# GpSimd's weight splits and stick-weight products cut into shorter instructions

## The chip, the cores and the metric

The kernel runs on one core of one Trainium2 chip. The metric is the device time of one execution in microseconds; the median of three runs before the change is 2070.41 us (2069.74 to 2076.77). Engines are named as the profile names them: PE is TensorE's matmul side, PEld its weight loads, DVE is VectorE, ACT is ScalarE, POOL is GpSimd, SP is SyncE. Lines such as L339 are lines of the kernel before.

## The reference

One decoder layer over 16 meta tokens and 1024 tokens of width 1024, all in float32:

```
xn   = rms_norm(h, g_pre_mix)
b, c, hc, q, k, v, g_conv, g_attn = split(xn @ w_in)            # 8 x 1024 columns
y    = b * causal_dwconv3(c * hc)
z    = q k^T / 8, strictly causal, 16 heads of 64
A[t,s] = sigmoid(z_ts) * prod_{s<j<t} (1 - sigmoid(z_tj))       # stick breaking
mix  = (sigmoid(g_conv + b0) * (y @ w_proj_conv) + sigmoid(g_attn + b1) * (A v @ w_proj_attn)) @ w_out
h    = h + rms_norm(mix, g_post_mix)
u, g = split(rms_norm(h, g_pre_ffn) @ w_up_gate)                # 2 x 2816 columns
out  = h + rms_norm((gelu(causal_dwconv3(u)) * g) @ w_down, g_post_ffn)
```

## The kernel before

Every product is computed to float32 accuracy from rounded operands: a tensor is split into `hi` (its rounded copy) and `lo` (what the rounding lost), and three matmuls, hi by hi, hi by lo and lo by hi, add up in one PSUM bank. The helper `split` (L63 to L65) does it: ACT copies the source into `hi`, and DVE, or POOL where it is named, subtracts `hi` from the source into `lo`.

The first stage, from about 75 to 1000 us, runs two things through one PE queue. One is the dense product `xn @ w_in`: 64 items of 128 output columns in the class `Dense`, each with three chunks of 342 tokens and 24 matmuls a chunk. `run(i)` first prepares the weights of item i+1 (`prep`, L102 to L110: the 128x1024 weight block `raw`, ACT's `whi`, POOL's `wlo`), asks for the DMA of item i+2, and then issues its own matmuls at L124 to L126. The same class later carries the 16 items of the two branch projections, so `prep` splits 80 weight blocks in all.

The other is the stick-breaking attention: 8 pairs of heads, and for each head three groups (g) of three query blocks of 114 rows. `stage1` (L311) handles the query blocks: a block sees nk = 128 + 114 b keys, b = 0 to 8. PE computes the scores z, ACT writes `fl` = sigmoid(-z/8) and `be` = sigmoid(z/8), and the closure `weights`, put off by one chunk through the list `late`, issues the rest: DVE's scan (L336) turns `fl` in place into the running product from the right, POOL multiplies `be` by it, shifted by one key (L339), POOL masks the last 114 columns (L340, an affine select) and fills a margin with zeros (L345, a memset). There are two buffers of `fl`, so block b+2's sigmoid waits until the product of block b has read its `fl`; there are six of `be`.

`stage2` (L353) consumes the three blocks of a group: PE transposes `be` by 128 keys (L373) into one of two PSUM tiles `tp`, ACT and DVE split it into `ah` and `al`, and PE multiplies these by the values (L363, L364). A transpose can only start when DVE has read the PSUM tile of two transposes earlier. A hand-written loop (L506 on) interleaves the steps of stage1, stage2 and the dense items by a table of costs; it fixes the order in which each engine gets its instructions. Engines work through their queues in that order. Beside these, DVE evacuates PSUM and computes the convolution branch (`conv3`: L197 on ACT, then L198 and L199 on DVE, 1026 columns each).

At the start (0 to 45 us) `start_items` normalises the nine token blocks (L459 on DVE for the first three, L461 on POOL and L462 on DVE for the others), transposes them (L179), and slips in the first two dense items, whose two `wlo` splits come between the second and the third token block.

Of the kernel before, what the change touches and what calls it, by code (L numbers as in the profile page):

```python
# [8 lines left out]
F32 = mybir.dt.float32  # L9
F32R = mybir.dt.float32r  # L10
AF = mybir.ActivationFunctionType
ALU = mybir.AluOpType
# [3 lines left out]
D = 1024  # L16
# [16 lines left out]
def block_kernel(ctx, tc, x, meta_tokens, g_pre_mix, w_in, channels, w_proj_conv,  # L33
                 w_proj_attn, w_out, g_post_mix, g_pre_ffn, w_up_gate, w_down,
                 g_post_ffn, out):
    nc = tc.nc
# [26 lines left out]
    def split(hi, lo, src, lo_engine=None):  # L63
        nc.scalar.copy(hi, src)  # L64
        (lo_engine or nc.vector).tensor_tensor(lo, src, hi.bitcast(F32), op=ALU.subtract)  # L65
# [14 lines left out]
    class Dense:  # L80
# [22 lines left out]
        def prep(self, i):  # L103
            if i < len(self.items) and i not in self.hl:
                self.load(i)
                raw = self.raw.pop(i)
                hi = wpool.tile([P, D], F32R, name="whi", tag="whi")
                lo = wpool.tile([P, D], F32R, name="wlo", tag="wlo")
                split(hi, lo, raw, nc.gpsimd)
                self.hl[i] = (hi, lo)  # L110

        def run(self, i):
# [198 lines left out]
    def stage1(p, h, g):  # L311
        res = []
        qh, ql, kk = QH[p][h], QL[p][h], KK[p][h]
        nk_end = P + QB * (3 * g + 2)
        for b in range(3 * g, 3 * g + 3):
            nk = P + QB * b
            q0 = QB * b
            fl = work.tile([P, NT], F32, name="fl", tag="fl")[:QB]
            be = work.tile([P, NT], F32, name="be", tag="be", bufs=6)[:QB]
            nch = -(-nk // 512)  # L320
            wch = 2 * (-(-nk // (2 * nch)))
            c0 = 0
            while c0 < nk:
                n = min(wch, nk - c0)
                z = ps_z.tile([P, 512], F32, name="z", tag="z")[:QB, :n]
                nc.tensor.matmul(z, qh[:, q0:q0 + QB], kk[:, c0:c0 + n], start=True, stop=False)
                nc.tensor.matmul(z, ql[:, q0:q0 + QB], kk[:, c0:c0 + n], start=False, stop=True)  # L327
                nc.scalar.activation(fl[:, c0:c0 + n], z, AF.Sigmoid, scale=-0.125)  # L328
                nc.scalar.activation(be[:, c0:c0 + n], z, AF.Sigmoid, scale=0.125)
                c0 += n  # L330
                if late:
                    late.pop(0)()
                if c0 < nk:
                    yield n
            def weights(fl=fl, be=be, nk=nk):
                nc.vector.tensor_tensor_scan(fl[:, :nk][:, ::-1], fl[:, :nk][:, ::-1],  # L336
                                             upper[:, NT - nk:][:, ::-1], 1.0,
                                             op0=ALU.mult, op1=ALU.max)
                nc.gpsimd.tensor_tensor(be[:, 0:nk - 1], be[:, 0:nk - 1], fl[:, 1:nk], op=ALU.mult)  # L339
                nc.gpsimd.affine_select(out=be[:, nk - QB:nk], in_=be[:, nk - QB:nk],  # L340
                                        pattern=[[-1, QB]], compare_op=ALU.is_gt, fill=0.0,
                                        base=0, channel_multiplier=1)
                pad = min(P * (-(-nk // P)), nk_end)
                if pad > nk:
                    nc.gpsimd.memset(be[:, nk:pad], 0.0)  # L345

            late.append(weights)
            res.append((be, nk))
            if len(res) == 3:
                units[(p, h, g)] = res  # L350
            yield n
# [676 lines left out]
    for k, _ in enumerate(products(0, *HALF[1], bank_of(ps_o, "po"), evac_u(*HALF[1]))):  # L1028
        if k % 2:
            next(prep, None)  # L1030
# [40 lines left out]
    for i in range(1, len(pairs)):  # L1071
        p, gate = divmod(i, 2)
        if gate:
            conv_gelu(p)
            sets = [products(i, 1, 512, bank, evac_g(p))]
        else:
            sets = [products(i, j0, n, bank, evac_u(j0, n)) for j0, n in HALF]
        for _ in prep:
            pass
        prep = prep_pair(i + 1) if i < last_pair else prep_down_first()  # L1080
        for si, st in enumerate(sets):
            for k, _ in enumerate(st):
                if gate or (7 * si + k) % 2:
                    next(prep, None)
# [45 lines left out]
    for gi, fbs in enumerate(groups):  # L1130
# [14 lines left out]
        for tb in range(8):  # L1145
# [3 lines left out]
            for hf in range(2):  # L1149
                ps = bank()  # L1150
                c = slice(hf * 512, (hf + 1) * 512)
# [6 lines left out]
                a = accs[tb][:, c]  # L1158
# [4 lines left out]
                if last:  # L1163
                    sq = dw.tile([P, 512], F32, name="sq", tag="sq", bufs=2)
                    nc.scalar.activation(sq, a, AF.Square, accum_out=ssqs[tb][:, hf:hf + 1])
                    eng = nc.vector if (tb == 7 and hf) else nc.gpsimd
                    eng.tensor_tensor(a, a, g_post2[:, c], op=ALU.mult)
            next(prep, None)
            if last:
                a, hb, s0 = accs[tb], hbs[tb], ssqs[tb]  # L1170
                nc.vector.tensor_tensor(s0[:, 0:1], s0[:, 0:1], s0[:, 1:2], op=ALU.add)
                r = rstd_of(fsml, s0[:, 0:1], P)
                for hf in range(2):
                    c = slice(hf * 512, (hf + 1) * 512)
# [60 lines left out]
```

## Time and profile before

| | us |
|---|---|
| median of three runs | 2070.41 |
| the profiled execution | 2079.27 |
| its span, first to last instruction | 2077.1 |
| PE busy | 1988.1 (96%) |
| PEld busy | 1860.9 (90%) |
| DVE busy | 1033.7 (50%) |
| ACT busy | 851.9 (41%) |
| POOL busy | 914.8 (44%) |
| POOL, 80 splits of `wlo` | 191.5 |
| POOL, 144 products of L339 | 178.3 |
| DVE, 144 scans of L336 | 228.0 |

Busy times are shares of one profiled execution, the slowest core's; there is one core. A matmul's recorded length (0.32 us for 342 columns) is its passage through the array, and its successor starts some 0.16 us after it, so an idle time recorded ahead of a matmul is a little shorter than the time that was lost. A row of the timeline gives start, length, engine, line, operation and tiles, and in brackets the engine's idle time before it with the work that ended it. The time that an instruction spends on waiting for a resource after it was started is part of its length, so two rows of one shape with different lengths are worth a look.

### The profile page before, as it was taken

The page shows a single profiled execution, that of the slowest core. Times are in us where ns is not written, and L with a number is a line of the kernel's source. Part 1 is how long each engine was busy: PE and PEld are TensorE (multiplying, and loading weights), DVE is VectorE, ACT ScalarE, POOL GpSimd, SP SyncE. Part 2 cuts the span into 40 slices and gives each one's busy share as a digit, 9 for nine tenths or more (in the row PEclk, how much of TensorE's full clock was granted, in tenths as well). Part 3 has the DMA queues.
Part 4 walks back from the last instruction along what each step waited for, and adds up shares of the span by engine and source line. Part 5 has one row for each costly group of instructions (what it writes and reads, how often), then busy time and mean ns, then how long its engine had stood idle before and what let it go on. Part 6 is the DMA issues. An engine that isn't in the chain of part 4 may idle for free.

```text
span 2077.1 us, 30701 instructions
## 1 busy us (share of the span) xinstructions
PE 1988.1 (96%) x12228; PEld 1860.9 (90%) x12228; DVE 1033.7 (50%) x1545; ACT 851.9 (41%) x1771; POOL 914.8 (44%) x764
## 2 busy tenths in 40 slices
PE   5999999999999999999999989979999999999997
PEld 5999999999999999999999989978898899878886
DVE  6445555555555555554232114685444444445546
ACT  4445454545444454545441113354334434412122
POOL 4444444434444444444212551225655656555353
PEclk9999999999999999999999999989999999999999
DMA  3111101111111101111475674313222122253323
GB/s 134 41 51 42 61 31 51 42 41 52 42 51 41 61 32 51 41 48 55 138 231 171 184 189 129 102 54 102 74 90 82 62 102 70 74 182 102 101 81 132
DMA packets 56171, 177.56 MB, mean 85 GB/s; under 512 B 12872, under 2 KB 12872, under 8 KB 56028
## 3 DMA queue, kind: packets, MB, share of 16 engines
q1 hardware_dynamic: 52704, 165.09, 24.5%
q10 hardware_dynamic: 3324, 10.50, 1.6%
q8 instruction: 96, 1.57, 0.3%
q14 instruction: 47, 0.39, 0.1%
HBM read 131.36 MB, written 44.21 MB: 85 GB/s over the span
## 4 chain that ended last, share of the span: by engine, by line
PE 74%; DVE 11%; DMA 6%; ACT 4%; POOL 3%; issue 2%; ACTq 0%; DVEq 0%; POOLq 0%; SPq 0%
PE mm L124 13%; PE mm L125 12%; PE mm L126 12%; PE st L863 6%; PE st L865 5%; PE st L867 5%; PE st L1157 3%; PE st L1155 3%; PE st L1156 3%; PE tp L373 3%; DVE fl L336 3%; PE av L363 2%; PE av L364 2%; DMA xv<-in_x_dram 2%; POOL a_op L65 2%
## 5 line engine op out<-in xcount | busy, mean ns | idle before, releaser
L124 PE MATMUL mm<-xnT,whi 128*128 128x342 f32 (+2 forms) x1536 | 506.8, 330 | 3.6 <-ACT xnT L64 3.6
L125 PE MATMUL mm<-xnT,whi 128*128 128x342 f32 (+2 forms) x1536 | 494.7, 322 | 0.5 <-DVE xnT L65 0.5
L126 PE MATMUL mm<-xnT,wlo 128*128 128x342 f32 (+2 forms) x1536 | 493.0, 321 | 0.0
L339 POOL TENSOR_TENSOR be<-be,fl 114x127 f32<-114x127 f32 (+2 forms) x144 | 178.3, 1238 | 372.3 <-DVE fl L336 350.9
L124 PEld LDWEIGHTS mm<-xnT,whi 128*128 128x128 f32 x1536 | 290.5, 189 | 8.3 <-ACT xnT L64 4.0
L125 PEld LDWEIGHTS mm<-xnT,whi 128*128 128x128 f32 x1536 | 291.1, 190 | 2.1 <-DVE xnT L65 1.0
L126 PEld LDWEIGHTS mm<-xnT,wlo 128*128 128x128 f32 x1536 | 290.5, 189 | 0.0
L336 DVE TENSOR_TENSOR_SCAN fl<-fl,upper 114x128 f32<-114x128 f32 (+2 forms) x144 | 228.0, 1585 | 117.6 <-ACT fl L328 102.8
L65 POOL TENSOR_TENSOR wlo<-raw,whi 128x1024 fp32r<-128x1024 f32 x80 | 191.5, 2394 | 203.5 <-ACT whi L64 203.5
L65 POOL TENSOR_TENSOR a_op<-raw,a_op 128x512 fp32r<-128x512 f32 (+1 forms) x136 | 193.6, 1436 | 88.6 <-ACT a_op L64 86.4
L65 DVE TENSOR_TENSOR al<-tp,ah 128x342 fp32r<-128x342 f32 (+4 forms) x288 | 127.3, 450 | 147.0 <-ACT ah L64 145.7
L64 ACT CAST ah<-tp 128x342 fp32r<-128x342 f32 (+4 forms) x288 | 112.7, 397 | 193.4 <-PE tp L373 185.1
L863 PE MATMUL st<-opT,a_op 128*128 128x258 f32 (+2 forms) x528 | 171.3, 324 | 2.3 <-ACT snap L878 1.1
L865 PE MATMUL st<-opT,a_op 128*128 128x258 f32 (+2 forms) x528 | 169.5, 321 | 2.4 <-DVE opT L65 1.5
L867 PE MATMUL st<-opT,a_op 128*128 128x258 f32 (+2 forms) x528 | 169.3, 321 | 0.0
L328 ACT ACTIVATE fl<-z 114x348 f32<-114x348 f32 (+10 forms) x240 | 111.3, 464 | 127.6 <-PE z L327 123.3
L64 ACT CAST a_op<-raw 128x512 fp32r<-128x512 f32 (+1 forms) x136 | 85.1, 633 | 152.6 <-DVE raw L775 46.0
L373 PE MATMUL tp<-ident,be 114*128 114x114 f32 x720 | 119.5, 263 | 27.7 <-DVE al L65 25.0
L1162 DVE TENSOR_TENSOR acc<-acc,st 128x512 f32<-128x512 f32 x144 | 98.5, 687 | 91.1 <-PE st L1157 91.1
L865 PE MATMUL st<-opB,a_op 128*128 128x512 f32 (+2 forms) x396 | 127.8, 323 | 1.8 <-DVE opB L65 1.8
L863 PE MATMUL st<-opB,a_op 128*128 128x512 f32 (+2 forms) x396 | 127.9, 323 | 0.0
L867 PE MATMUL st<-opB,a_op 128*128 128x512 f32 (+2 forms) x396 | 127.4, 322 | 0.0
(171 smaller groups left out, 4327.6 us busy)
## 6 DMA issues: line engine op xcount, KB each, us to landing
raw<-in_w_in_dram SPq DMA_DIRECT2D x64, 512.0 KB, 3.4
raw<-in_w_up_gate_dram SPq DMA_DIRECT2D x44, 512.0 KB, 3.5
act_d<-owork SPq DMA_DIRECT2D x22, 512.0 KB, 4.2
araw<-act_d SPq DMA_DIRECT2D x22, 512.0 KB
raw<-in_w_down_dram SPq DMA_DIRECT2D x22, 512.0 KB, 3.2
y_d<-yy SPq DMA_DIRECT2D x8, 513.0 KB
ga_d<-gt SPq DMA_DIRECT2D x8, 513.0 KB
o_d<-ot SPq DMA_DIRECT2D x8, 513.0 KB
```

The costliest lines, as they stand in the source:

```text
L64: nc.scalar.copy(hi, src)
L65: (lo_engine or nc.vector).tensor_tensor(lo, src, hi.bitcast(F32), op=ALU.subtract)
L124: nc.tensor.matmul(ps, wh, xh, start=(kb == 0), stop=False)
L125: nc.tensor.matmul(ps, wh, xl, start=False, stop=False)
L126: nc.tensor.matmul(ps, wl, xh, start=False, stop=(kb == KB - 1))
L328: nc.scalar.activation(fl[:, c0:c0 + n], z, AF.Sigmoid, scale=-0.125)
L336: nc.vector.tensor_tensor_scan(fl[:, :nk][:, ::-1], fl[:, :nk][:, ::-1], upper[:, NT - nk:][:, ::-1], 1.0, op0=ALU.mult, op1=ALU.max)
L339: nc.gpsimd.tensor_tensor(be[:, 0:nk - 1], be[:, 0:nk - 1], fl[:, 1:nk], op=ALU.mult)
L373: nc.tensor.transpose(tp[:n, QB * j:QB * (j + 1)], blocks[j][0][:, kb * P:kb * P + n], ident[:QB, :QB])
L863: nc.tensor.matmul(ps, wt[:, 0, k], xh, start=start and kb == 0, stop=False, skip_group_check=True)
L865: nc.tensor.matmul(ps, wt[:, 0, k], xl, start=False, stop=False, skip_group_check=True)
L867: nc.tensor.matmul(ps, wt[:, 1, k], xh, start=False, stop=stop and kb == 3, skip_group_check=True)
```

## The change

Two places, both on POOL's queue. In `Dense.prep` the subtraction into `wlo`, one instruction of 128x1024, becomes four of 128x256 in the same place of the queue; ACT's copy into `whi` stays whole. In `weights` the product `be * fl` over nk-1 columns becomes as many instructions of equal width as keep each at 384 columns or fewer: one for 127, 241 and 355 columns, two for 469, 583 and 697 (235, 292 and 349 wide at most), three for 811, 925 and 1039 (271, 309 and 347). Nothing else changes: the same elements are computed from the same operands, with 80 x 3 = 240 and 16 x (3 x 1 + 3 x 2) = 144 instructions more on POOL.

```
-                split(hi, lo, raw, nc.gpsimd)
+                nc.scalar.copy(hi, raw)
+                for a in range(0, D, 256):
+                    c = slice(a, a + 256)
+                    nc.gpsimd.tensor_tensor(lo[:, c], raw[:, c], hi[:, c].bitcast(F32),
+                                            op=ALU.subtract)
...
-                nc.gpsimd.tensor_tensor(be[:, 0:nk - 1], be[:, 0:nk - 1], fl[:, 1:nk], op=ALU.mult)
+                w = -(-(nk - 1) // (-(-nk // 384)))
+                for a in range(0, nk - 1, w):
+                    e = min(a + w, nk - 1)
+                    nc.gpsimd.tensor_tensor(be[:, a:e], be[:, a:e], fl[:, a + 1:e + 1],
+                                            op=ALU.mult)
```

## The prediction

> **What bounds the kernel now.** I read the page first, then PE's waits, then the timeline around those waits on all engines.
>
> ```profile
> span 2077.1 us, 30701 instructions
> PE 1988.1 (96%) x12228; PEld 1860.9 (90%) x12228; DVE 1033.7 (50%) x1545; ACT 851.9 (41%) x1771; POOL 914.8 (44%) x764
> ```
>
> PE is the bound nearly everywhere. POOL, the engine that is changed, is idle more than half of the span, so its work matters only where somebody waits for it, or is held up by it. PE's waits say who that is:
>
> ```profile
> PE tp L373 <- DVE al L65: 25.0, 22, 2.0
> PE tp L179 <- DVE xn L459: 18.1, 3, 9.5
> ...
> PE mm L126 <- POOL wlo L65: 2.7, 3, 1.2
> PE tp L373 <- DVE vv L65: 2.4, 6, 0.4
> ```
>
> The columns are total us, times, longest us. PE waits for POOL itself only three times. In the attention stage it waits 28 times for DVE to read a transposed PSUM tile, 27.4 us in all: that is about all the idle time of this stage, and the most that can be won there. So the question is why DVE, busy half of the time, is late. The longest of the stalls that repeat once per pair of heads:
>
> ```profile
> 235.48 2.39 POOL L65 TENSOR_TENSOR wlo<-raw,whi 128x1024 fp32r<-128x1024 f32 x1
> ...
> 240.19 2.02 POOL L339 TENSOR_TENSOR be<-be,fl 114x1039 f32<-114x1039 f32 x1 [1.44 <-DVE fl L336]
> ```
> ```profile
> 235.70 4.34 DVE L336 TENSOR_TENSOR_SCAN fl<-fl,upper 114x1040 f32<-114x1040 f32 x1 [1.61 <-ACT fl L328]
> ```
> ```profile
> 238.71 0.32 PE L126 MATMUL mm<-xnT,wlo 128*128 128x342 f32 x1
> 240.51 0.51 PE L373 MATMUL tp<-ident,be 114*128 114x114 f32 x3 [1.48 <-DVE al L65]
> ```
>
> The scan reads two SBUF tensors. It was started at 235.70, while POOL's weight split ran (235.48 to 237.87), and ended at 240.04: 2.17 us after the split's end. So it stood still for the rest of the split, 2.17 us, and then needed its own 2.17. The `al` behind it in DVE's queue came late, and PE's matmuls, which follow each other by 0.16 us, stood from 238.87 to 240.51: 1.64 us lost. The second stall of each pair:
>
> ```profile
> 218.18 2.40 POOL L65 TENSOR_TENSOR wlo<-raw,whi 128x1024 fp32r<-128x1024 f32 x1
> ```
> ```profile
> 218.79 2.87 DVE L198 SCALAR_TENSOR_TENSOR yy<-cc,par,yy 128x1026 f32<-128x1026 f32 x1 [1.47 <-ACT yy L197]
> ...
> 222.00 1.27 DVE L199 SCALAR_TENSOR_TENSOR yy<-cc,par,yy 128x1026 f32<-128x1026 f32 x1
> 223.20 0.57 DVE L65 TENSOR_TENSOR al<-tp,ah 128x228 fp32r<-128x228 f32 x2
> ```
> ```profile
> 220.57 0.32 PE L124 MATMUL mm<-xnT,whi 128*128 128x342 f32 x1
> 222.14 0.30 PE L373 MATMUL tp<-ident,be 114*100 114x114 f32 x1 [1.25 <-DVE al L65]
> ...
> 223.64 0.38 PE L364 MATMUL av<-al,vv 128*128 128x228 f32 x1
> ```
>
> L198 and L199 have the same shape; the one that met a split took 2.87 us, the other 1.27. PE lost 222.14 - 220.73 = 1.41 us. Both stalls have one cause: a DVE instruction with two SBUF inputs and a POOL instruction that reads SBUF do not run together, and the split holds DVE up for as long as its rest lasts.
>
> **Does the chip hand over between two POOL instructions?** Shorter instructions help only if DVE gets its turn while POOL has more of them queued. Two places show it:
>
> ```profile
> 274.00 1.21 POOL L339 TENSOR_TENSOR be<-be,fl 114x583 f32<-114x583 f32 x1 [1.38 <-ACT be L329]
> 275.28 1.47 POOL L340 TENSOR_SCALAR_AFFINE_SELECT be<-be 114x114 f32<-114x114 f32 x1
> ...
> 1336.97 2.48 POOL L65 TENSOR_TENSOR opB<-xr,opB 128x1032 fp32r<-128x1032 f32 x1 [6.10 <-ACT opB L64]
> 1339.40 3.13 POOL L65 TENSOR_TENSOR mb<-mraw,mb 128x912 fp32r<-128x912 f32 x1
> ```
> ```profile
> 274.55 2.12 DVE L336 TENSOR_TENSOR_SCAN fl<-fl,upper 114x698 f32<-114x698 f32 x1
> ...
> 1337.11 3.41 DVE L738 SCALAR_TENSOR_TENSOR xv<-row,s,g_pre 114x1024 f32<-114x1024 f32 x1
> ```
>
> The scan of 274.55 ended at 276.67, 1.46 us after the product's end, and POOL's mask, queued right behind the product, ended at 276.75: DVE went first. At 1339.45 the same happened between two subtractions of one line: L738 ended at 1340.52, 1.07 us after the first, and the second came out at 1342.53. So the turn passes to DVE at an instruction's end, and POOL waits in its turn.
>
> **The change part by part.** What a piece costs:
>
> ```profile
> L65 POOL TENSOR_TENSOR wlo<-raw,whi 128x1024 fp32r<-128x1024 f32 x80 | 191.5, 2394 | 203.5 <-ACT whi L64 203.5
> ...
> L339 POOL TENSOR_TENSOR be<-be,fl 114x811 f32<-114x811 f32 x16 | 26.0, 1622 | 56.0 <-DVE fl L336 55.8
> ...
> L339 POOL TENSOR_TENSOR be<-be,fl 114x355 f32<-114x355 f32 x16 | 13.0, 814 | 1.5
> L339 POOL TENSOR_TENSOR be<-be,fl 114x241 f32<-114x241 f32 x16 | 10.4, 649 | 1.1
> ...
> L65 POOL TENSOR_TENSOR w_o<-raw,w_o 128x352 fp32r<-128x352 f32 x1 | 0.9, 886 | 5.3 <-ACT w_o L64 5.3
> ```
>
> No 256-column piece is in the trace. From below it costs a quarter of 2394 ns, 0.60 us; from above the 352-column row, 0.89. The straight line through both rows gives (2394 - 886)/672 = 2.24 ns a column and 0.67 us, which I take. Four make 2.68 us, 0.29 more than now. For L339, (1622 - 649)/570 = 1.71 ns a column leaves 0.24 us for each instruction, so 811 columns in three pieces of 0.70 last 2.10 instead of 1.62. In all POOL gets 80 x 0.29 + 144 x 0.24 = 58 us more, hidden in its idle 56%; if that cover failed, they would show as waits for `be` or `wlo`.
>
> The scan stall: the split's first piece ends at 235.48 + 0.67 = 236.15, the scan then runs until 238.32 instead of 240.04. That is 1.72 us earlier, more than the 1.64 that PE lost, so this stall goes; what is next behind it, two `al` of half a microsecond, has no wait now. Seven such stalls, one in each pair but the first: 7 x 1.64 = 11.5 us. What it delays: three pieces wait until 238.32 and end at 240.33, and the last product of the group, which ends at 242.21 now, comes behind them and a memset of some 0.95 us, at about 243.7. Its reader is far off:
>
> ```profile
> 251.90 0.46 PE L373 MATMUL tp<-ident,be 114*128 114x114 f32 x3
> ```
>
> 9.7 us of slack shrink by 1.5 and by PE's 1.64: nobody waits.
>
> The convolution stall: the first piece ends at 218.85, L198 runs 1.27 us to 220.12, the `al` after it is ready by 220.6 instead of 222.08. But L199 follows, and now meets the second piece: it starts at 220.79, ends at 222.06, and the two `al` behind it end at 222.63, 1.14 us earlier than now. PE, 1.41 earlier, finds them late by 0.3 at the matmul that stands at 223.64. So about 1.0 of 1.41 is won, 7 times: 7.0 us.
>
> The start of the kernel:
>
> ```profile
> 13.82 4.67 POOL L65 TENSOR_TENSOR wlo<-raw,whi 128x1024 fp32r<-128x1024 f32 x2 [8.38 <-ACT whi L64]
> ```
> ```profile
> 16.42 2.09 DVE L77 TENSOR_TENSOR s<-s,t 128x1 f32<-128x1 f32 x1
> 18.54 3.33 DVE L459 SCALAR_TENSOR_TENSOR xn<-xt,s,gb 128x1024 f32<-128x1024 f32 x1
> ```
>
> A one-column operation waits 2 us for a split, and L459 misses its turn and waits again for L461. In pieces, L77 goes at 16.50 and L459, after one more piece, ends near 18.6 instead of 21.87. PE has a gap there (18.1 us of waits for L459 in the table), but POOL's first L461 moves 2.2 us later behind the postponed pieces. Between 0 and 3.3 us; I take 2.5, since the next use of that L461 is after the same PE work that comes earlier.
>
> At 0 I take what may go either way: the other stalls of the table (the six waits for `vv`, six more short ones, the first pair's; 0 to 8 us won), PE's three direct waits for `wlo` (0.9 lost if it waits for all four pieces, 2.7 won if for the first alone). Against it I set 1 us for DVE instructions that meet a piece where they met nothing before; the bound is 0.67 us at each of two tight places in eight pairs, 10.7 us.
>
> Sum: 11.5 + 7.0 + 2.5 - 1.0 = 20 us. Of the profiled execution's 2079.27 (span 2077.1) that leaves 2059.3; its runs' median was 2070.41, 8.9 below it, and I carry the 20 us over unchanged: 2050.4 us.
>
> **The rivals.**
>
> A: a wait for `fl` takes over. A scan that slips in between two pieces of the product of the block before keeps that product's `fl` busy for longer, and ACT writes the same buffer soon after:
>
> ```profile
> 345.88 1.62 POOL L339 TENSOR_TENSOR be<-be,fl 114x811 f32<-114x811 f32 x1
> ```
> ```profile
> 347.61 2.19 DVE L336 TENSOR_TENSOR_SCAN fl<-fl,upper 114x926 f32<-114x926 f32 x1 [1.47 <-POOL be L339]
> ```
> ```profile
> 348.74 0.46 ACT L328 ACTIVATE fl<-z 114x348 f32<-114x348 f32 x1 [0.78 <-PE z L327]
> ```
>
> The scan comes 1.73 us after the product's start. With pieces of 0.70 the third is under way by then (from 1.40), and ACT, at 2.86, finds the product done at 2.10. Over 0.87 us a piece, the scan goes first and the product ends at 1.73 + 2.19 + 0.87 = 4.79: ACT is held 1.93 us, PE's scores and transposes behind it. Eight such blocks, 15.4 us, leave a gain of 4 or so: 2066, no change. The 241 and 355 rows (0.65, 0.81) speak against it. Chance 0.12.
>
> B, slower: the turn does not pass within a train of like pieces. Its place is the same two stalls and the start; DVE then waits for the whole train, which has become longer. With p for a piece the loss is 14 x (4p - 2.39) + (8p - 4.67) = 64p - 38.1: 4.8 us at 0.67, 18.9 at 0.89; from p = 0.76 it is more than 0.5%. At 0.78 it is 11.8 us: 2082. The hand-over at 1339.45 speaks against it, though that instruction pair had different operands. The Trainium skill bears on this (GPSIMD Engine Reference, section 2.1 Instruction dispatch): its cores do not wait for each other between instructions, each begins the next as soon as its own share is done; by that rule there might be no moment between two pieces at which the port is free. The two hand-overs shown above do not agree with that reading. Chance 0.07.
>
> C: the won time is half given back at the next `al`, as with L199 above, at each of the tight places: 2070.4 - 9.5 = 2061, within 0.5%, barely. For it speaks that DVE runs several two-input instructions close together there; against it that `al` reads one PSUM and one SBUF tensor and met POOL's work at 240 us without being longer. Chance 0.09.
>
> **How the numbers follow.** The forecast has 0.72, A 0.12, C 0.09, B 0.07. I count as no change what lies within 0.5%, 10.4 us, about what a measurement of this kernel can tell. Faster: the forecast but for its weak end, and a part of C, 0.73. Same: A, most of C, that weak end, 0.20. Slower: B, 0.07. The forecast's own range: with the 8 us of the other stalls and the 2.7 it wins 31, 2040; with all 10.7 against it it wins 10, 2060. The range goes on to A, 2068, and leaves out B and the extremes.
>
> **What would show it.** In the new profile the scans of 1040 columns should last under 3 us instead of 4.3 and L198 under 2.2; PE's waits for `al` should fall from 25.0 us to under 8; the pieces should show lengths near 0.67 and 0.70, some stretched by a scan between them; the third token block's L459 should end before 20 us. Waits of ACT's `fl` for POOL's `be` would show A; scans that outlast a whole train, B; the same total of waits for `al` in more and shorter pieces, C. The forecast is wrong if PE's idle time in the attention stage falls by less than 10 us.

## The result, and the profile after

The changed kernel took 2050.32 us (median of four runs, 2047.77 to 2053.06) beside 2073.59 for the kernel before (four runs): a ratio of 0.9886, 95% interval 0.9854 to 0.9918. In a later measurement it was 2048.63 beside 2070.40, ratio 0.9889 (0.9859 to 0.9919). So the change wins some 22 us, 1.1%; the forecast was 2050.4.

From here on line numbers are those of the kernel shown: four or eight lines were added, so L124 to L126 became L128 to L130, the scan L336 became L340, the product L339 became L346, and so on. The page of the changed kernel, its totals:

```profile
span 2046.2 us, 31035 instructions
PE 1981.9 (97%) x12228; PEld 1858.8 (91%) x12228; DVE 1010.1 (49%) x1545; ACT 852.5 (42%) x1771; POOL 1038.5 (51%) x1148
```

The same PE work in 31 us less of span, with POOL 124 us busier, waiting for its turn included. What PE waited for (total us, times, longest us):

```profile
PE tp L183 <- DVE xn L467: 15.2, 3, 9.3
...
PE mm L128 <- DVE gal L623: 5.6, 1, 5.6
...
PE tp L381 <- DVE al L65: 3.8, 6, 2.2
...
PE tp L381 <- DVE vv L65: 0.2, 1, 0.2
```

The 28 waits for DVE at the transposes, 27.4 us before, are seven of 4.0 us together. The groups of instructions (count, busy us, mean ns) show why, first in the kernel before, then in the changed kernel:

```profile
L336 DVE TENSOR_TENSOR_SCAN fl<-fl,upper 114x1040 f32<-114x1040 f32 x16 | 51.4, 3215 | 16.4 <-ACT fl L328 16.2
...
L198 DVE SCALAR_TENSOR_TENSOR yy<-cc,par,yy 128x1026 f32<-128x1026 f32 x8 | 22.3, 2790 | 12.0 <-ACT yy L197 12.0
```
```profile
L340 DVE TENSOR_TENSOR_SCAN fl<-fl,upper 114x1040 f32<-114x1040 f32 x16 | 39.9, 2494 | 16.4 <-ACT fl L332 16.2
...
L202 DVE SCALAR_TENSOR_TENSOR yy<-cc,par,yy 128x1026 f32<-128x1026 f32 x8 | 11.3, 1408 | 11.8 <-ACT yy L201 11.8
```

The scan of 1040 columns now takes 2494 ns on the mean instead of 3215. The two tight places in the timeline of the changed kernel:

```profile
216.66 1.40 DVE L202 SCALAR_TENSOR_TENSOR yy<-cc,par,yy 128x1026 f32<-128x1026 f32 x1 [1.47 <-ACT yy L201]
217.97 0.50 DVE L65 TENSOR_TENSOR al<-tp,ah 128x342 fp32r<-128x342 f32 x1
218.40 1.34 DVE L203 SCALAR_TENSOR_TENSOR yy<-cc,par,yy 128x1026 f32<-128x1026 f32 x1
...
232.13 2.37 DVE L340 TENSOR_TENSOR_SCAN fl<-fl,upper 114x1040 f32<-114x1040 f32 x1 [1.60 <-ACT fl L332]
```
```profile
232.05 0.28 POOL L348 TENSOR_SCALAR_AFFINE_SELECT be<-be 114x114 f32<-114x114 f32 x1
232.29 2.74 POOL L112 TENSOR_TENSOR wlo<-raw,whi 128x256 fp32r<-128x256 f32 x1
```

L202 takes 1.40 us where it took 2.87. The scan had its turn behind the mask of 0.28 us; the first piece, ready at 232.29, lasts 2.74 us, because it waits until the scan is through at 234.50. The wait has moved from DVE, whom PE needs, to POOL, whom nobody needs at this moment.

How far this carries is best seen from a landmark: the transposes of `be`, whose first and last start (89.8 to 1013.1) frame the attention stage. The rows give the shortest, median and longest in ns, then first and last start; the kernel before, its second profile, the changed kernel, its second profile:

```profile
L373 PE MATMUL tp<-ident,be x720: 257/261/318, 89.8 to 1013.1; 114*128 114x114 f32 x168, 114*58 114x114 f32 x4, 114*16 114x114 f32 x4, 114*100 114x114 f32 x4
```
```profile
L373 PE MATMUL tp<-ident,be x720: 258/261/319, 88.5 to 1011.9; 114*128 114x114 f32 x168, 114*58 114x114 f32 x4, 114*16 114x114 f32 x4, 114*100 114x114 f32 x4
```
```profile
L381 PE MATMUL tp<-ident,be x720: 258/261/319, 87.2 to 984.0; 114*128 114x114 f32 x168, 114*58 114x114 f32 x4, 114*16 114x114 f32 x4, 114*100 114x114 f32 x4
```
```profile
L381 PE MATMUL tp<-ident,be x720: 257/261/397, 86.3 to 985.7; 114*128 114x114 f32 x168, 114*58 114x114 f32 x4, 114*16 114x114 f32 x4, 114*100 114x114 f32 x4
```

The last transpose comes 1012.5 - 984.9 = 27.6 us earlier (means of two). That is 6 us more than the medians won. So up to there more was won than forecast. These four executions show no loss behind it: from the last transpose to the end of the span they take 1064.0 and 1061.8 us before, 1062.2 and 1062.4 after. But both executions of the kernel before (2079.27 and 2075.85 us) were slower than its median of some 2070; by the medians, something was given back, and the experiments look for it.

### The profile page after: what moved, and what is told of

It is laid out like the page before. It is cut to its first block, busy times and chain, and to the rows that moved or that the text cites. A ratio compares the mean times of both kernels' runs of the same rounds, so it can differ in the third digit from the quotient of the medians.

```text
span 2046.2 us, 31035 instructions
## 1 busy us (share of the span) xinstructions
PE 1981.9 (97%) x12228; PEld 1858.8 (91%) x12228; DVE 1010.1 (49%) x1545; ACT 852.5 (42%) x1771; POOL 1038.5 (51%) x1148
## 4 chain that ended last, share of the span: by engine, by line
PE 81%; DVE 7%; POOL 4%; DMA 3%; ACT 2%; issue 2%; ACTq 0%; DVEq 0%; POOLq 0%; SPq 0%
PE mm L128 14%; PE mm L129 13%; PE mm L130 13%; PE st L871 5%; PE st L875 5%; PE st L873 5%; PE tp L381 3%; PE st L1165 3%; PE st L1163 3%; PE st L1164 3%; POOL a_op L65 2%; PE av L371 2%; PE av L372 2%; PE z L331 2%; PE z L330 2%
## 5 line engine op out<-in xcount | busy, mean ns | idle before, releaser
L128 PE MATMUL mm<-xnT,whi 128*128 128x342 f32 (+2 forms) x1536 | 506.9, 330 | 3.6 <-ACT xnT L64 3.6
L130 PE MATMUL mm<-xnT,wlo 128*128 128x342 f32 (+2 forms) x1536 | 492.9, 321 | 0.0
L112 POOL TENSOR_TENSOR wlo<-raw,whi 128x256 fp32r<-128x256 f32 x320 | 268.8, 872 | 184.7 <-ACT whi L109 183.7
L346 POOL TENSOR_TENSOR be<-be,fl 114x271 f32<-114x271 f32 (+14 forms) x288 | 205.4, 734 | 261.3 <-DVE fl L340 253.9
L128 PEld LDWEIGHTS mm<-xnT,whi 128*128 128x128 f32 x1536 | 290.4, 189 | 8.3 <-ACT xnT L64 4.1
L130 PEld LDWEIGHTS mm<-xnT,wlo 128*128 128x128 f32 x1536 | 290.3, 189 | 0.0
L340 DVE TENSOR_TENSOR_SCAN fl<-fl,upper 114x128 f32<-114x128 f32 (+2 forms) x144 | 214.4, 1490 | 115.9 <-ACT fl L332 79.4
```

Source lines behind the costliest of these rows:

```text
L112: nc.gpsimd.tensor_tensor(lo[:, c], raw[:, c], hi[:, c].bitcast(F32), op=ALU.subtract)
L128: nc.tensor.matmul(ps, wh, xh, start=(kb == 0), stop=False)
L130: nc.tensor.matmul(ps, wl, xh, start=False, stop=(kb == KB - 1))
L346: nc.gpsimd.tensor_tensor(be[:, a:e], be[:, a:e], fl[:, a + 1:e + 1], op=ALU.mult)
```

## The experiments

Each median stands beside the kernel before in the same measurement: 2071.92 us for the rows from "splits only" to "splits in halves", 2070.40 for "splits in eighths" to "start whole" and the second of "changed", 2070.07 for the last three and the second profile of the kernel before, which is a single run of 2075.85. "Last transpose" is the landmark above; "to the projection's end" is the time from it to the first matmul of the output projection (`po`), the stage in which PE is fed by the DMAs of gates and weights.

| kernel | median us | ratio (95%) | last transpose | to the projection's end |
|---|---|---|---|---|
| before, two profiles | | | 1013.1, 1011.9 | 241.2, 230.3 |
| changed, two profiles | 2050.32, 2048.63 | 0.9886, 0.9889 | 984.0, 985.7 | 237.5, 239.8 |
| splits only | 2053.42 | 0.9907 (0.9891-0.9923) | 988.3 | 232.6 |
| products only | 2071.00 | 0.9992 (0.9979-1.0004) | 1012.6 | 230.9 |
| memsets for splits | 2037.88 | 0.9831 (0.9815-0.9847) | 979.4 | 229.9 |
| splits in halves | 2062.53 | 0.9952 (0.9935-0.9970) | 999.8 | 231.0 |
| splits in eighths | 2043.24 | 0.9857 (0.9826-0.9889) | 982.6 | 235.4 |
| products at 128 | 2056.60 | 0.9920 (0.9895-0.9946) | 996.7 | 235.5 |
| start whole | 2047.29 | 0.9895 (0.9852-0.9938) | 986.4 | 234.2 |
| projection whole | 2042.34 | 0.9860 (0.9840-0.9880) | 985.8 | 230.3 |
| sized by place | 2044.51 | 0.9861 (0.9840-0.9883) | 982.4 | 233.0 |
| more pieces | 2038.90 | 0.9850 (0.9822-0.9877) | 978.1 | 230.9 |

**One part alone.** The kernel before with only the first hunk of the diff, and with only the second.

> Only the weight splits are cut in four; the stick-weight products stay whole. Theory 1 (a DVE instruction with two SBUF inputs stands still while a GpSimd instruction that reads SBUF runs, and the whole weight split was what it met at the two tight places of each pair): nearly all of the gain, 20 to 27 us below the kernel before, PE's waits for al under 6 us instead of 25.0, scans of 1040 columns near 2.5 us. Rival (the products' cut gives a good part of it, because it lets the scans in earlier): at most 14 us below the kernel before, and PE's waits for al at 10 us or more.

> Only the stick-weight products are cut (at most 384 columns each); the weight splits stay whole. Theory 1: the stalls behind the weight splits all stay, so within 3 us of the kernel before, PE's waits for al between 22 and 28 us, scans of 1040 columns still at 4.3 us where they meet a split. Rival: 8 us or more below the kernel before. A third way, the cut alone costs something because fl is read for longer: up to 5 us above it.

The splits alone win 18.5 us, the products alone 0.9, which is no difference. PE's waits for `al`, splits only and then products only:

```profile
PE tp L377 <- DVE al L65: 7.5, 10, 2.0
```
```profile
PE tp L377 <- DVE al L65: 24.4, 16, 2.1
```

So the weight splits are the cause. Two numbers missed: 18.5 is below the 20 expected, though the attention stage won 24.2 (1012.5 - 988.3), and waits of 7.5 us are left where 6 was the limit. Beside the cut splits the products' cut is worth something after all: 988.3 against 984.9, 3.4 us up to the last transpose. Five of the ten waits left with splits only, 0.84 to 0.86 us each, stand behind a scan of 698 columns that meets a whole product of 583 columns. With the splits only such a scan takes 2.48 us, with the products only 1.59:

```profile
381.49 2.48 DVE L340 TENSOR_TENSOR_SCAN fl<-fl,upper 114x698 f32<-114x698 f32 x1
```
```profile
275.31 1.59 DVE L336 TENSOR_TENSOR_SCAN fl<-fl,upper 114x698 f32<-114x698 f32 x1
```

The products alone take away six waits of half a microsecond (16 are left of 22), but the long ones become longer (scans of 1040 columns 3335 ns instead of 3215), so that nothing of it is seen in the time.

**Length, or reading?** Theory 1 says that it is the reading of SBUF; an instruction that only writes should hold nobody up. So memsets of about the same length stand in for the subtraction; this kernel leaves out the weights' low parts.

```
-                split(hi, lo, raw, nc.gpsimd)
+                nc.scalar.copy(hi, raw)
+                nc.gpsimd.memset(lo.bitcast(F32), 0.0)
+                nc.gpsimd.memset(lo.bitcast(F32), 0.0)
+                nc.gpsimd.memset(lo[:, 0:512].bitcast(F32), 0.0)
```

> The weight split's subtraction is replaced by three memsets of the same tile (1024, 1024 and 512 columns, some 2.4 us together), which read nothing; the products stay whole. This leaves out the weights' low parts: all matmuls still run, on zeros in their place. Theory 1 (it is the reading of SBUF that holds DVE up): no scan and no convolution step is longer for meeting a memset, PE's waits for al fall under 5 us, 20 to 30 us below the kernel before. Rival (any GpSimd instruction holds DVE up while it runs, and a shorter one for less): scans that meet a memset of 0.95 us are longer by up to 0.95 us, and part of the stalls stays: 8 to 18 us below.

It won 34.0 us. POOL's and DVE's timeline at the place of the scan's stall:

```profile
228.34 0.95 POOL L110 MEMSET wlo<- 128x1024 f32 x1
229.36 0.95 POOL L111 MEMSET wlo<- 128x1024 f32 x1
```
```profile
228.52 2.33 DVE L339 TENSOR_TENSOR_SCAN fl<-fl,upper 114x1040 f32<-114x1040 f32 x1 [1.61 <-ACT fl L331]
```

The scan runs right across both memsets in 2.33 us, and all sixteen take 2.32 or 2.33 here (mean 2325 ns): this is its length when nothing holds it up. The rival, by which any GpSimd instruction holds DVE up, falls. Of the 34.0 us, 33.1 are won by the last transpose (1012.5 - 979.4). Why it is 4 us beyond the expected 30 is not shown; a memset waits neither for ACT's copy nor for the weight's DMA, and what this is worth was not measured apart.

The Trainium skill says this of the chip (SBUF — State Buffer, section Who interferes with whom): a VectorE instruction with two SBUF inputs contends with a GpSimd instruction that reads SBUF, not with one that only writes it. The two timelines agree: 4.34 us across a subtraction, 2.33 across memsets.

**Length of a piece.** The range in the first hunk with 512 columns a piece, and with 128; the products stay whole in both.

> The weight splits in two pieces of 512 columns (some 1.3 us each); the products stay whole. Theory 1: what is won goes by how long the rest of a piece lasts. The 1040-column scan would end 1.1 us earlier instead of 1.7, which leaves 0.5 of each 1.64 us stall; the convolution's second step meets the second half in full, so of that stall between nothing and 0.9 us is won; 1.5 us at the start. Sum 9 to 16 us, about 11 below the kernel before. Rival (that there is a second instruction at all is what counts, as DVE gets in between): 20 us or more, as with four pieces.

> The weight splits in eight pieces of 128 columns; the products stay whole, so this stands beside the run with four pieces and whole products (2053.4 us). Theory 1: the rest of a piece that DVE has to wait for halves again, to at most some 0.4 us, but four pieces had already taken all but 7.5 us of PE's waits for al: within 5 us of four pieces, 2048 to 2056. Rival (every further instruction on GpSimd costs PE something, by its own 0.2 us or by the turns that it takes from DVE): 2060 or more.

Whole, halves, quarters and eighths put the last transpose at 1012.5, 999.8, 988.3 and 982.6. The mean length of the 1040-column scan, halves and then quarters (products whole in both):

```profile
L340 DVE TENSOR_TENSOR_SCAN fl<-fl,upper 114x1040 f32<-114x1040 f32 x16 | 45.0, 2813 | 16.4 <-ACT fl L332 11.4 <-POOL be L344 4.8
```
```profile
L340 DVE TENSOR_TENSOR_SCAN fl<-fl,upper 114x1040 f32<-114x1040 f32 x16 | 40.9, 2557 | 16.4 <-ACT fl L332 11.4 <-POOL wlo L112 4.8
```

Against 2325 ns unhindered that is 0.49 and 0.23 us of hold-up; the kernel before had 3215 - 2325 = 0.89, and the eighths, at 2487 ns, have 0.16. The gain goes by the rest of a piece. The halves won 9.4 us, within 9 to 16, and their rival, which wanted 20, falls. The gain did not run out at four pieces, as I had expected: the eighths came out at 2043.2, 5 us under the range. They won 27.2 us where the quarters won 18.5. By the last transpose 5.7 of these 8.7 us are there, since PE's waits for `al` fell from 7.5 to 2.4; the other 3 lie behind it and are not explained.

**The rival by `fl`.** The divisor 384 in the second hunk became 128.

> The changed kernel with the stick-weight products in pieces of at most 128 columns (up to nine) instead of 384. By rival A of the prediction a scan then goes in between the pieces of the product before it and fl comes free late: 811 columns in seven pieces of some 0.43 us are at the fifth when the scan comes after 1.73 us; the last two end near 4.9 us after the start where ACT wants the buffer at 2.86, which holds ACT and PE by some 2 us in eight blocks: 10 to 18 us slower than the changed kernel, with ACT's wait for POOL's be in the tens of us. Against it: ACT and PE have other work to do meanwhile, and it stays within 4 us of the changed kernel.

It is 8.0 us slower than the changed kernel in the same measurement, the last transpose 996.7 against 985.7. ACT's waits at `fl` that POOL's product ended, this kernel first, then the changed kernel (second profile):

```profile
ACT fl L332 <- POOL be L346: 43.1, 26, 2.7
```
```profile
ACT fl L332 <- POOL be L346: 7.6, 9, 1.1
```

Rival A is a real mechanism: with a long train of short products, scans slip in, `fl` comes free late and ACT stands. The last transpose is 11.0 us later, which is within the 10 to 18 that I had worked out; the median is only 8.0 slower. At 384 columns it hardly begins: all of ACT's waits at `fl`, whoever ended them, are 126.7 us in the kernel before, 127.4 in the changed kernel and 144.6 here.

**The start.** In the first hunk the width was `D if i < 2 else 256`.

> The changed kernel with the first two weight splits whole again, those of the start; all others in four. The step of the prediction for the start says 2.5 us (0 to 3.3): the third token block's L459 ends near 21.9 us again instead of 18.9, and the dense items begin 2 to 3 us later. If the start is not on the path, no difference in the first dense item after 80 us.

The third token block's L468 is back at 3.33 us and ends at 21.59:

```profile
18.26 3.33 DVE L468 SCALAR_TENSOR_TENSOR xn<-xt,s,gb 128x1024 f32<-128x1024 f32 x1
```

The first transpose of `be` starts at 89.1 against 87.2 and 86.3, so 1.9 to 2.8 us are won by then. At the last transpose 0.7 to 2.4 are left, and in the medians (2047.29 against 2048.63) nothing can be seen of them.

**What is given back, and where.** The same two kernels once more, for second profiles:

> The changed kernel once more, for a second profile on this chip. The first profile won 29 us up to the end of the attention stage, and only 21.6 us of it show in the medians. If the loss is chance in the projection stage (a wait of 5.6 us for a gate tile's DMA with a slow stretch of TensorE's clock behind it), this profile has the same 28 to 30 us up to the end of attention and a wait at another place or of another length. If the change itself brings it on, the wait of 5 us or more stands there again.

> The kernel before once more, for a second profile. Its first profile had waits of 2.7 us for wlo and 5.2 us for a gate tile in the projection stage with a slow stretch of TensorE's clock behind them, and ran 8.9 us above its median. If that was chance, this profile shows less of it and a span of 2066 to 2071 with the attention stage as before, and PE's waits for al at 24 to 26 us.

The changed kernel shows the long wait again: `PE mm` waited 6.1 us for `gal`, a tile of the gates. Up to the last transpose it won 26.8 us (1012.5 - 985.7), a little under the expected 28 to 30. The kernel before does not show the wait again (0.3 us instead of 5.2): 230.3 us for the stretch instead of 241.2, and 25.0 us of waits for `al` as before. Its span of 2073.7 still missed the expected 2066 to 2071, because it lost time elsewhere: from the first `po` to the end it took 831.5 us, and the first profile 822.8. What differs in the changed kernel is seen at SP, whose queue issues the weights' DMAs. From 1100 us to the stage's end, waits of the queue at the line that loads `w_out`, before and then changed:

```profile
SPq L640 <- POOL wlo L65: 14.5, 7, 2.5
```
```profile
SPq L648 <- POOL wlo L112: 17.4, 7, 2.9
```

The weight buffer is free only when the split has read it, and four pieces last 2.8 us instead of 2.4; in this stage, where no scan runs, the cut has only this price. How 0.4 us a block becomes a wait of 5 us at PE is not shown, and the price does not simply follow this wait: the eighths have 21.3 us of it and a stretch of 235.4. The test:

> The changed kernel with the 16 weight splits of the branch projections whole again; those of the first stage in four. Both profiles of the changed kernel lose up to 6 us in the projection stage against the other kernels: the next weight block's DMA waits there for a buffer that the split frees, and a split in four takes 2.79 us instead of 2.39. If that is the cause, PE's longest wait for gal there (5.6 and 6.1 us) falls under 3 us and the time by 3 to 7 us, to 2042 to 2046. If it is the DMAs' own scatter, the wait is anything from 0 to 6 us again and the time within 3 us of the changed kernel's 2048.6.

```
-                for a in range(0, D, 256):
-                    c = slice(a, a + 256)
+                w = 256 if i < 64 else D
+                for a in range(0, D, w):
+                    c = slice(a, a + w)
```

2042.34 us, in the range of the first reading; the stretch takes 230.3 us, and the wait for `gal` is 0.4. In the table, the six profiles with splits in quarters or eighths there have 232.6 to 239.8, mean 235.8; six of the seven with whole splits or memsets have 229.9 to 233.0, mean 230.9, and the seventh, 241.2, is the first profile of the kernel before (the halves have 231.0). The difference is 4.9 us without that seventh profile and 3.5 with it. Another reckoning takes each kernel's median less its last transpose: 1059.9 to 1066.3 us with quarters or eighths there, mean 1062.6; 1056.5 to 1062.1 with whole splits or memsets, mean 1059.0. So some 3 to 5 us are likely given back, on top of a scatter of up to 11 us that has nothing to do with the change, as the two profiles of the kernel before show. The intervals of the two ratios overlap (0.9840 to 0.9880, 0.9859 to 0.9919); the price is likely, its size is not settled.

**Better versions.** Pieces by place: 256 columns for the two splits of the start, 128 for the rest of the first stage, whole in the projections. Then the same with the start's products and two late sorts of splits in four.

> Pieces sized by place: 256 columns for the two splits of the start, 128 for the other 62 of the first stage, whole in the projections; products as in the changed kernel. Eight pieces with whole products won 30.0 us up to the end of attention although they lost 2 at the start against four; the products' cut was worth 4 us beside four pieces. Theory 1: 32 to 35 us up to the end of attention, at most 2 us of waits for al left, 2038 to 2043. Rival (GpSimd runs short of time or fl comes free late with both cuts): no better than 2043.

> The kernel with pieces sized by place, and three more sorts of GpSimd instruction cut in four: the start's products xn (1024 columns), the late splits of mb (912) and of the operands opB and the like (1024 and 1032). In the profile before these held up L75 at 37.5 us by 2.2 us and L738 at 1337 us by 2.1. Theory 1: 2 to 5 us at the start and 1 to 3 us around 1340 us, 3 to 7 us below the kernel with pieces sized by place. If DVE's hold-ups at these places are hidden: within 2 us of it.

The first wins 30.1 us up to the last transpose, not 32, 2.5 us of waits for `al` are left where 2 was the limit, and its 2044.5 lies on the rival's side of the line; its stretches behind the attention were slower than those of the kernel with whole projections. The second has the lowest median of the versions that compute everything: 2038.90 us, ratio 0.9850, interval 0.9822 to 0.9877, 5.6 us below the first (3 to 7 were expected) and 4.3 us earlier at the last transpose (978.1), won at the start, where the first transpose comes at 82.5 instead of 86.9. Around 1340 us nothing was won: PE's wait of 6.8 us for `xv` stands there as before. Between the versions from 2038.9 to 2044.5 the intervals overlap, so their order is not settled.

## Why the prediction was right, point by point

The mechanism was right: DVE instructions with two SBUF inputs stood behind a reading GpSimd instruction, and the turn passes at an instruction's end, within a train of like pieces too (rival B did not happen: L202's 1.40 us across a train).

The sum was right by luck, by two misses that nearly cancel: more was won in the attention stage than reckoned, and something was given back behind it.

- The scan's stall, 11.5 us, and the convolution's, 7.0: won; none of these fourteen waits is left. I had let 0.4 of each 1.41 us come back at L199; L203 took 1.34 instead of 1.27 and nothing of that came back at 220 us. The seven waits of the convolution were 8.5 us, 9.6 with the 0.16 us that go with each, so 2.6 more than I took. The scan's own length is 2.33 us, not the 2.17 that I read off behind the split; little hung on that.
- "The other stalls", taken at 0 with a bound of 8 us: this is the step that failed. The table of waits falls by 23.4 us, and with 0.16 us each for some 21 waits that are gone by 26.8; some 6.5 of these are other stalls. Of the six for `vv` five are gone and one is 0.16 us, of the six of half a microsecond four are gone and two are 0.33. The waits for `vv` came from a scan of 584 columns behind a split; here it is before and after:

```profile
271.62 2.23 DVE L336 TENSOR_TENSOR_SCAN fl<-fl,upper 114x584 f32<-114x584 f32 x1
```
```profile
266.78 1.36 DVE L340 TENSOR_TENSOR_SCAN fl<-fl,upper 114x584 f32<-114x584 f32 x1
```

Those of half a microsecond came from the scan of 698 columns that met a whole product (2.12 us at 274.55, 1.59 with the products only, where none of the six is left). I had used that scan as proof of the hand-over and not counted its stall.
- The 1 us set against new meetings was about right; six waits for `al` are left, 3.8 us, of which 2.2 are the first pair's and 0.5 stand at two new places.
- The start, 2.5 us: the third token block's L467 ends at 18.91, before 20 as forecast; 1.9 to 2.8 us are won at the first transpose, but at most 2.4 at the last.
- PE's waits for `wlo`, taken at 0 between -0.9 and +2.7: the changed kernel has none or one of 0.6 us, but the kernel before has none in its second profile either, so nothing was won there. The price was elsewhere, in the DMA that waits for the buffer. I had looked at who waits for `wlo` and not at who waits for `raw`. Likely some 3 to 5 us lost.
- POOL's busy time: 58 us more by the sum, 124 in the trace. The splits rose from 191.5 to 268.8 us, of which 320 x 0.738 = 236 is about their own length; the rest is time in which they wait for DVE, which counts as theirs, and the masks rose for the same reason from 72.9 to 93.4. The cover held all the same.
- A piece: 0.67 us estimated, 0.738 in the median of the trace.

```profile
L112 POOL TENSOR_TENSOR wlo<-raw,whi x320: 724/738/2750, 13.7 to 1203.8; 128x256 fp32r<-128x256 f32 x160
```

- The 8.9 us between the profiled execution and the median were carried over unexplained. The projection stage of that one execution accounts for them (241.2 us against 230.3 in the second profile), so a sum against that execution's own time would have been misled in just that stage.
- Rival C did not happen. Rival A exists and begins at finer products, as its condition (a scan that arrives before the last piece is under way) said; its price was 8.0 to 11.0 us at 128 columns, where I had reckoned 15.4 for pieces of 0.87 us.

## What to carry to other kernels

Where two engines share a way to memory and take turns by whole instructions, cut the instructions of the engine that has time, and cut them where the other one's work is on the path: here most of the gain comes from the 62 splits of the attention stage, while the 16 that meet no scan only held a buffer for longer. Ask of a longer train not only who reads its result, but who waits for what it reads. And work out the short stalls with the same cause as the long ones: here they were a quarter of what PE's waits fell by.

## What the runs showed of the hardware

The runs of one kernel scatter, from 2067 to 2078 us in 17 runs of the kernel before, and the profiles show this scatter behind the attention stage. The last transpose of two profiles of one kernel differs by 1.2 us before and 1.7 after. The stretch to the projection's end lies between 229.9 and 241.2 us in the fourteen profiles, and the rest, from the first `po` on, between 821.1 and 831.5.

A wait of PE of 5 us or more in the projection stage is followed by a slower clock. The changed kernel's windows (length, busy us of PE, PEld, DVE, ACT and POOL, then the granted clock, DMA share, GB/s) around the wait that ends at 1211.97:

```profile
1205.00:1212.00 7.00, 1.39 (x10) 1.11 (x8) 0.97 (x4) 1.60 (x4) 3.04 (x3) 0.81 0.90 229
1212.00:1220.60 8.60, 8.60 (x43) 8.60 (x44) 1.82 (x5) 1.01 (x3) 4.95 (x6) 0.76 0.69 162
1220.70:1227.50 6.80, 6.80 (x46) 6.80 (x45) 3.11 (x4) 1.57 (x4) 2.20 (x2) 1.00 0.43 91
```

By an estimate from these rows, a clock of 0.76 over 8.6 us costs some 2 us more than the wait itself (8.6 x 0.24). After the waits of 5.2 us (kernel before) and 6.1 (changed, second profile) the clock was 0.50 for some 4 us; after 3.0 (eighths) it was 0.68; after 2.4 (splits only) and 0.4 (projection whole) it stayed at 1.00. What decides the DMAs' length from run to run stays open.
